# Four stage edits in a one-core decoder block: branch weights pair by pair, half of the merged columns kept on chip, partial sums added where they form, Strassen pairs moved

## The chip, the core and the metric

The kernel runs on one core of a Trainium2 chip. A core has a matrix engine (PE, TensorE), a vector engine (DVE), an activation engine (ACT), GpSimd (POOL), a queue engine (SP) that here only issues DMAs, an on-chip memory (SBUF) and the matmul's accumulators (PSUM). Each engine runs its own instruction stream in order; semaphores tie the streams together. The metric is the device time of one execution in microseconds; the median of several runs counts.

## The reference

One layer of a hybrid decoder, 256 tokens, width 2048, float32. What the change touches is the second half of it:

```python
gates = jax.nn.sigmoid(gz + b_gate[l]).reshape(B, S, N_BRANCH, D_MODEL)
mixed = gates[:, :, 0] * (branches[0] @ w_branch[l, 0])
for n in range(1, N_BRANCH):
    mixed = mixed + gates[:, :, n] * (branches[n] @ w_branch[l, n])
h = h + mixed @ w_out[l]
v = rms_norm(h, norm_ffn[l])
h = h + (jax.nn.silu(v @ w_ffn_gate[l]) * (v @ w_ffn_up[l])) @ w_ffn_down[l]
return rms_norm(h, norm_final)
```

Ahead of it the input is normed and projected (`w_in`), and four token mixers (two attentions, a linear recurrence, a windowed attention) give the four `branches`, each 256 x 512. `w_branch` is 4 x 512 x 2048, `w_out` 2048 x 2048, `w_ffn_gate` and `w_ffn_up` 2048 x 5632, `w_ffn_down` 5632 x 2048.

## The kernel before

**Numbers.** Each float32 operand is split into a high and a low part (`whi`, `wlo` for weights, `yh`, `yl` and the like for activations), and a product is three matmuls: high weight with high activation, low with high, high with low. A weight piece is 256 rows x 512 columns, loaded as `raw` by SP, its high part made by ACT (`whi<-raw`), its low part by DVE (`wlo<-raw,whi`). Four buffers each of `raw`, `whi` and `wlo` go round (`wpiece`, line 118).

**`pair`** (line 245) multiplies the 256 tokens (two row halves t) with two 512-column weight blocks (wl, wr) and walks the contraction in pairs kp of 128-row blocks. A normal kp is 8 products, 24 matmuls. A kp listed in `skps` is done as one Strassen step: 7 products, 21 matmuls, but `s_weights` (line 220) then forms sums of the weights first: four adds of 128x512 (`se`, `sx`), a high part (`sh`, `seh`, ACT) and a low part (`sl`, `sel`, DVE). Four of its products gather in their own banks p1, p5, p6, p7; at the last Strassen kp they are put together as the partial sum `u` (lines 284 to 291). The plain products gather in q0 and q1. With `split=n` the last n normal kps are held back and written product by product for the four outputs one after the other (lines 297 to 307), pinned in that order by `keep_in_program_order`. `small_banks` puts the four outputs in p1, p5, p7, p6 instead of q0 and q1.

**Stages.** From about 427 us on six times a gate block (`pair` on `w_in`, 8 kps) and a branch block (`pair` on `w_branch`, two kps, line 813) alternate; DVE multiplies gate and branch and adds to `mixed`. Then `w_out` in two column halves (line 864), 11 blocks of gate and up projection of the FFN (line 887, f = 0 to 10), the down projection `w_fd` in two halves cc (line 932, 22 kps each) and the final norm. Between stages, 128x128 transposes on PE turn a result round (`trans_bank`). The transposed `mixed` goes out to DRAM through `nat_out` (`mrg`, issued by POOL) and comes back in `m_split` (`mload`, issued by SP) as the activations `mth`, `mtl` of `w_out`. Such work is put in the list `later` and written out by `run_later`, at kp 1 of the next `pair` (line 272) or at its last Strassen kp.

**Order.** The code is written under a tile scheduler, which orders each engine's stream itself; only what is pinned keeps its place. So the order in the streams is not that of the code.

Of the kernel before, what the change touches and what calls it, by code (L numbers as in the profile page):

```python
# [10 lines left out]
AF = mybir.ActivationFunctionType  # L11
# [6 lines left out]
NKT = D // P  # L18
# [11 lines left out]
def hybrid_block_kernel(  # L30
# [213 lines left out]

    def pair(wl, wr, nkp, skps, a_of, upool=None, split=0, small_banks=False):

# [24 lines left out]
        for kp in range(nkp):  # L271
            if kp == 1 and (not skps or skps[0] > 1) and not small_banks:
                run_later()
            blk, sums = a_of(kp, kp in skps)
            if kp in skps:
# [525 lines left out]
    for n, cc in ((2, 0), (0, 0), (1, 1), (3, 1), (2, 1), (0, 1)):  # L801
# [5 lines left out]
        for t in range(2):  # L807
# [5 lines left out]
        pp, _ = pair(w_branch[n, :, col:col + 512], w_branch[n, :, col + 512:col + 1024], 2, (),  # L813
                     a_tiles(*ys[n]), split=2, small_banks=True)
        for i in range(2):
            if n == 1:
                mixed_of[2 * cc + i] = gp.tile([P, 2, 512], F32, tag="mixed", name="mixed")
        for t in range(2):
            for i in range(2):
                g, m = gate[:, 2 * t + i, :], mixed_of[2 * cc + i][:, t, :]  # L820
                tt(m if n == 1 else g, g, pp[t][i], ALU.mult)
                if n != 1:
                    tt(m, m, g, ALU.add)
        if n == 0:
            for i in range(2):
                later.append(lambda c=2 * cc + i: nat_out(mixed_of[c], merged, f"mrg{c}_"))
    s2.close()
# [17 lines left out]
    m_of = a_tiles(mth, mtl)  # L845

    def m_split(kp, s):
        if kp % 2 == 0:
            late["m"] = fp.tile([P, 2, 512], F32, tag="hd", name="mload")
        v = late["m"][:, kp % 2, :]  # L850
        nc.sync.dma_start(v, merged[kp])
        h, lo = (t[:, 2 * kp:2 * kp + 2, :].rearrange("p a b -> p (a b)") for t in (mth, mtl))
        act(h, v)
        tt(lo, v, rd(h), ALU.subtract)
        return m_of(kp, s)

# [28 lines left out]
    for f in range(DFF // 512):  # L885
        fs = slice(f * 512, (f + 1) * 512)
        q, u = pair(w_fg[:, fs], w_fu[:, fs], NKT // 2, (3, 5) if f == 0 else FS if f % 2 else (0, 3, 5), v_of, fp, split=1)
        hd = fp.tile([P, 2, 512], F32, tag="hd", name="hd")
        for t in range(2):
            o = u[:, 2 * t:2 * t + 2, :]  # L890
            tt(o, o, q[t], ALU.add)
            act(u[:, 2 * t, :], u[:, 2 * t, :], AF.Silu, scale=rstd2[:, t:t + 1])

        tt(hd, u[:, 0:4:2, :], u[:, 1:4:2, :], ALU.mult)
        later.append(lambda hd=hd, f=f: nat_out(hd, hid, f"hid{f}_"))
# [9 lines left out]
    ah = uv.tile([P, 4, 2, 2 * S], F32R, tag="tl", name="ah")  # L905
    DS = (3, 6, 9, 12, 15)

# [22 lines left out]
    for cc in range(2):  # L930
        cs = slice(cc * 1024, (cc + 1) * 1024)
        q, u = pair(w_fd[:, cc * 1024:cc * 1024 + 512], w_fd[:, cc * 1024 + 512:(cc + 1) * 1024], NFT // 2, DS,
                    lambda kp, ws: h_of(cc, kp, ws), fp, split=2 if cc else 1)
        for t in range(2):
            o = hn[:, t, cs].rearrange("p (a b) -> p a b", a=2)
            stt(o, u[:, 2 * t:2 * t + 2, :], rstd2[:, t:t + 1], o, ALU.mult, ALU.add)
        for t in range(2):
# [61 lines left out]
```

## Time and profile before

| | before |
|---|---|
| median of three runs | 1542.94 us (1542.46, 1542.94, 1548.3) |
| profiled execution, its own time | 1541.55 us |
| its span, first to last instruction | 1539.8 us |
| PE busy | 97% of the span |
| DVE, ACT, POOL busy | 77%, 53%, 5% |
| mean granted TensorE clock | 0.992 of full speed |

The rows are read with these names: `q<-whi,ah` is a matmul into bank q with weight piece `whi` and activation `ah`; `[1.41 <-DVE wlo L60]` behind a row says that the engine sat idle 1.41 us before it, and that the last thing it waited for was DVE's `wlo`. Line 216 is every matmul of `pair`, line 60 every two-operand DVE instruction, line 57 every ACT instruction, so rows are told apart by their tiles. A matmul of 512 columns lasts 0.39 us in the rows, but the next one starts before it ends: the pace is the distance of starts. Where PE is nearly always busy, time is found in the places where this distance is larger.

### The profile page before, as it was taken

How to read it: one execution, taken by the hardware profiler on the slowest of the kernel's cores; microseconds unless marked ns; L12 is line 12 of the kernel's file. 1: busy time of each engine (PE TensorE's matmuls, PEld its weight loads, DVE VectorE, ACT ScalarE, POOL GpSimd, SP SyncE). 2: the span in 40 equal slices, each digit the busy share in tenths (PEclk: the TensorE clock that was granted, in tenths of full speed). 3: DMA queues.
4: the chain of work that ended last, by engine and by line, in shares of the span. 5: the costliest groups of instructions: out<-in, count | busy, mean ns of one | idle time of the engine just before them, and what ended most of it. 6: DMA issues, size and time to landing. Idle time of an engine off the chain costs nothing.

```text
span 1539.8 us, 18550 instructions
## 1 busy us (share of the span) xinstructions
PE 1499.9 (97%) x6772; PEld 1231.3 (80%) x6772; DVE 1193.1 (77%) x1391; ACT 820.4 (53%) x947; POOL 76.7 (5%) x99
## 2 busy tenths in 40 slices
PE   8999999999999999998998999999999999999997
PEld 7878888887877877786887888888888888887885
DVE  5756645769679668765567989999999999898775
ACT  5555844545444444443465655564555556664643
POOL 4000300001000000000000000000000000001001
PEclk9999999999999999999999999999999999999999
DMA  7655555567566666666657567666766668876663
GB/s 237 214 150 158 154 172 159 171 176 255 167 196 208 222 201 196 191 184 219 225 177 246 177 195 256 199 215 193 234 200 220 201 221 269 280 263 216 212 209 110
DMA packets 159499, 313.64 MB, mean 204 GB/s; under 512 B 10736, under 2 KB 12848, under 8 KB 159280
## 3 DMA queue, kind: packets, MB, share of 16 engines
q1 hardware_dynamic: 155104, 298.92, 61.7%
q0 software_dynamic: 4272, 13.54, 2.5%
q8 instruction: 53, 0.87, 0.2%
q14 instruction: 38, 0.31, 0.1%
q10 hardware_dynamic: 32, 0.01, 0.0%
HBM read 302.46 MB, written 9.96 MB: 203 GB/s over the span
## 4 chain that ended last, share of the span: by engine, by line
PE 89%; DVE 3%; issue 3%; DMA 2%; ACT 1%; POOL 0%; SPq 0%; POOLq 0%; ACTq 0%; DVEq 0%
PE q L216 51%; PE acc L133 20%; PE p L216 14%; PE ps L165 2%; DMA sx<-in_w_in_dram 1%; DVE wlo L60 1%; DVE sl L60 1%; ACT sh L57 1%; DMA mload<-mrg 0%; DMA xq<-in_x_dram 0%; PE ps L533 0%; PE ps L729 0%; PE ps L552 0%; DMA fin<-hid 0%; PE ps L491 0%
## 5 line engine op out<-in xcount | busy, mean ns | idle before, releaser
L60 DVE TENSOR_TENSOR wlo<-raw,whi 128x1024 fp32r<-128x1024 f32 (+1 forms) x418 | 510.1, 1225 | 216.7 <-ACT whi L57 213.7
L57 ACT ACTIVATE whi<-raw 128x1024 fp32r<-128x1024 f32 (+1 forms) x418 | 438.2, 1050 | 438.1 <-PE q L216 252.8
L133 PE MATMUL acc<-wlo,uth 128*128 128x512 f32 (+1 forms) x448 | 173.4, 390 | 0.0
L133 PE MATMUL acc<-whi,utl 128*128 128x512 f32 (+1 forms) x448 | 173.4, 388 | 0.0
L133 PE MATMUL acc<-whi,uth 128*128 128x512 f32 (+1 forms) x448 | 168.0, 391 | 0.6 <-DVE nat L64 0.4
L216 PE MATMUL q<-whi,ah 128*128 128x512 f32 x512 | 161.1, 392 | 3.0 <-DVE hn L68 2.5
L216 PE MATMUL q<-whi,vth 128*128 128x512 f32 x408 | 159.6, 392 | 0.0
L216 PE MATMUL q<-wlo,vth 128*128 128x512 f32 x408 | 159.0, 390 | 0.0
L216 PE MATMUL q<-whi,vtl 128*128 128x512 f32 x408 | 158.7, 391 | 0.0
L57 ACT ACTIVATE sh<-sx 128x2048 fp32r<-128x2048 f32 x59 | 112.9, 1914 | 82.2 <-issue 34.6
L60 DVE TENSOR_TENSOR sl<-sx,sh 128x2048 fp32r<-128x2048 f32 x59 | 135.0, 2287 | 26.3 <-ACT sh L57 26.3
L216 PEld LDWEIGHTS q<-whi,ah 128*128 128x128 f32 x512 | 96.8, 189 | 24.1 <-DVE hn L68 3.0
L216 PE MATMUL q<-whi,uth 128*128 128x512 f32 x288 | 112.5, 394 | 2.4 <-DVE gate L60 2.4
L216 PE MATMUL q<-wlo,uth 128*128 128x512 f32 x288 | 113.2, 393 | 0.0
L216 PE MATMUL q<-whi,utl 128*128 128x512 f32 x288 | 112.7, 391 | 0.0
L60 DVE TENSOR_TENSOR sel<-se,seh 128x1536 fp32r<-128x1536 f32 x59 | 103.4, 1752 | 7.8 <-ACT seh L57 7.8
L57 ACT ACTIVATE seh<-se 128x1536 fp32r<-128x1536 f32 x59 | 87.3, 1480 | 36.4 <-DVE se L60 36.2
L216 PE MATMUL q<-wlo,ah 128*128 128x512 f32 x256 | 100.3, 392 | 0.0
L133 PEld LDWEIGHTS acc<-wlo,uth 128*128 128x128 f32 x448 | 84.6, 189 | 16.9 <-issue 1.0
L133 PEld LDWEIGHTS acc<-whi,utl 128*128 128x128 f32 x448 | 84.5, 189 | 16.4 <-issue 0.7
L133 PEld LDWEIGHTS acc<-whi,uth 128*128 128x128 f32 x448 | 82.1, 189 | 16.9 <-issue 0.7
L216 PEld LDWEIGHTS q<-whi,vtl 128*128 128x128 f32 x408 | 76.6, 188 | 15.9
(384 smaller groups left out, 2531.8 us busy)
## 6 DMA issues: line engine op xcount, KB each, us to landing
raw<-in_w_in_dram SPq DMA_DIRECT2D x168, 512.0 KB, 3.6
raw<-in_w_ffn_down_dram SPq DMA_DIRECT2D x68, 512.0 KB, 5.1
raw<-in_w_ffn_gate_dram SPq DMA_DIRECT2D x51, 512.0 KB, 3.8
raw<-in_w_ffn_up_dram SPq DMA_DIRECT2D x51, 512.0 KB, 4.6
sx<-in_w_ffn_up_dram SPq DMA_DIRECT2D x37, 512.0 KB, 3.9
sx<-in_w_ffn_gate_dram SPq DMA_DIRECT2D x37, 512.0 KB, 4.8
raw<-in_w_branch_dram SPq DMA_DIRECT2D x32, 512.0 KB, 4.3
raw<-in_w_out_dram SPq DMA_DIRECT2D x32, 512.0 KB, 4.7
```

Of the source, the lines that this page charges most:

```text
L57: return nc.scalar.activation(o, i, f, **kw)
L60: return (eng or nc.vector).tensor_tensor(out=o, in0=a, in1=b, op=op)
L133: m = nc.tensor.matmul(acc, x_, w_, start=st, stop=sp_)
L165: nc.tensor.transpose(pt[:, i * S + t * P:i * S + (t + 1) * P], nat[:, t, (c0 + i) * P:(c0 + i + 1) * P], ident)
L216: m = nc.tensor.matmul(acc, x_, w_, start=st, stop=sp_)
```

## The change

It has five parts.

1. The branch block drops `split=2`: its two kps are written kp by kp, and nothing there is pinned any more.
2. Merged columns 2 and 3 (`mixed_of[2]`, `mixed_of[3]`, ready last) no longer go through DRAM: `to_T` transposes them and writes `mth` and `mtl` straight from PSUM (`mth<-ps`, `mtl<-ps`), and `m_split` returns them for kp 4 to 7. From `w_out` on, `run_later` comes at kp 2 instead of kp 1.
3. The first FFN block, f = 0, has no Strassen kp any more (before: kp 3 and 5). Its result then is only in q: ACT applies Silu from PSUM and DVE multiplies with the other half.
4. The two `pair`s on `w_fd` get a sixth Strassen kp, 18.
5. `hn` gets the partial sum `u` where `u` is formed (`at_mid`) instead of behind the `pair`.

```diff
-    late = {"psum": None, "turn": 0}
+    late = {"psum": None, "turn": 0, "at": 1}
...
-            if kp == 1 and (not skps or skps[0] > 1) and not small_banks:
+            if kp == late["at"] and (not skps or skps[0] > kp) and not small_banks:
                 run_later()
...
                     tt(u[:, 1:4:2, :], p[5].unsqueeze(1).to_broadcast([P, 2, 512]), u[:, 1:3, :], ALU.subtract)
+                    if at_mid is not None:
+                        at_mid(u)
                     run_later()
...
         pp, _ = pair(w_branch[n, :, col:col + 512], w_branch[n, :, col + 512:col + 1024], 2, (),
-                     a_tiles(*ys[n]), split=2, small_banks=True)
+                     a_tiles(*ys[n]), small_banks=True)
...
-        if n == 0:
-            for i in range(2):
-                later.append(lambda c=2 * cc + i: nat_out(mixed_of[c], merged, f"mrg{c}_"))
+        if n == 0 and cc == 0:
+            for c in range(2):
+                later.append(lambda c=c: nat_out(mixed_of[c], merged, f"mrg{c}_"))
...
+    for c in (2, 3):
+        later.append(lambda c=c: to_T(mixed_of[c], mth, mtl, 4 * c))
+
     def m_split(kp, s):
+        if kp > 3:
+            return m_of(kp, s)
...
+    late["at"] = 2
...
-        q, u = pair(w_fg[:, fs], w_fu[:, fs], NKT // 2, (3, 5) if f == 0 else FS if f % 2 else (0, 3, 5), v_of, fp, split=1)
+        q, u = pair(w_fg[:, fs], w_fu[:, fs], NKT // 2, () if f == 0 else FS if f % 2 else (0, 3, 5), v_of, fp, split=1)
...
+        if u is None:
+            for t in range(2):
+                act(hd[:, t, :], q[t][:, 0, :], AF.Silu, scale=rstd2[:, t:t + 1])
+                tt(hd[:, t, :], hd[:, t, :], q[t][:, 1, :], ALU.mult)
...
-    DS = (3, 6, 9, 12, 15)
+    DS = (3, 6, 9, 12, 15, 18)
...
+        def at_mid(u):
+            for t in range(2):
+                o = hn[:, t, cs].rearrange("p (a b) -> p a b", a=2)
+                stt(o, u[:, 2 * t:2 * t + 2, :], rstd2[:, t:t + 1], o, ALU.mult, ALU.add)
+
...
-                    lambda kp, ws: h_of(cc, kp, ws), fp, split=2 if cc else 1)
-        for t in range(2):
-            o = hn[:, t, cs].rearrange("p (a b) -> p a b", a=2)
-            stt(o, u[:, 2 * t:2 * t + 2, :], rstd2[:, t:t + 1], o, ALU.mult, ALU.add)
+                    lambda kp, ws: h_of(cc, kp, ws), fp, split=2 if cc else 1, at_mid=at_mid)
```

Up to the first branch block the streams of all engines are the same. PE has as many instructions as before (6688): six matmuls more in f = 0, three fewer in each `w_fd` pair. Four DMAs less are issued by POOL (`mrg`) and four less by SP (`mload`).

**PE, first branch block, before.** p1, p5, p7, p6 are the four outputs; pieces 4070 and 4076 are the left and right block of kp 0, 4082 and 4088 those of kp 1. The block's 4th to 9th matmul:

```order
L216 MATMUL p1_4064<-whi_4070,yh_2536 128x512
L216 MATMUL p1_4064<-wlo_4071,yh_2536 128x512
L216 MATMUL p1_4064<-whi_4070,yl_2537 128x512
L216 MATMUL p1_4064<-whi_4082,yh_2536 128x512
L216 MATMUL p1_4064<-wlo_4083,yh_2536 128x512
L216 MATMUL p1_4064<-whi_4082,yl_2537 128x512
```

The first matmul on a kp 1 piece is the 7th of the block, the first on its low part the 8th.

**PE, first branch block, after** (4070 and 4076 as before, 4106 and 4112 are the pieces of kp 1), the block's 22nd to 30th matmul:

```order
L216 MATMUL p6_4067<-whi_4076,yh_2536 128x512
L216 MATMUL p6_4067<-wlo_4077,yh_2536 128x512
L216 MATMUL p6_4067<-whi_4076,yl_2537 128x512
L216 MATMUL p1_4064<-whi_4106,yh_2536 128x512
L216 MATMUL p5_4065<-whi_4112,yh_2536 128x512
L216 MATMUL p7_4066<-whi_4106,yh_2536 128x512
L216 MATMUL p6_4067<-whi_4112,yh_2536 128x512
L216 MATMUL p1_4064<-wlo_4107,yh_2536 128x512
L216 MATMUL p1_4064<-whi_4106,yl_2537 128x512
```

A kp 1 piece is now first read by the 25th matmul, its low part by the 29th. DVE's stream around it is the same as before up to the low parts of kp 1.

**DVE, start of `w_out`, before.** `mixed_4566` is merged column 3, `mload_5773` and `mload_5884` the reloaded halves for kp 0 and 1, and for kp 2 and 3; `wlo_5891` and `wlo_5897` are the low parts of kp 2's weights, `wlo_5857` of kp 1's:

```order
L60 TENSOR_TENSOR wlo_5857<-raw_5854,whi_5856 128x1024
L60 TENSOR_TENSOR mixed_4566<-mixed_4566,u_5583 128x512
L60 TENSOR_TENSOR mtl_5766<-mload_5773,mth_5765 128x512 x2
L60 TENSOR_TENSOR wlo_5891<-raw_5888,whi_5890 128x1024
L60 TENSOR_TENSOR wlo_5897<-raw_5894,whi_5896 128x1024
L60 TENSOR_TENSOR mtl_5766<-mload_5884,mth_5765 128x512
```

**The same place after** (`wlo_5825` belongs to kp 1, `wlo_5887` and `wlo_5893` to kp 2, `mload_5880` to kp 2 and 3):

```order
L60 TENSOR_TENSOR wlo_5825<-raw_5822,whi_5824 128x1024
L60 TENSOR_TENSOR mixed_4566<-mixed_4566,u_5583 128x512
L60 TENSOR_TENSOR mtl_5766<-ps_5852,mth_5765 128x512
L60 TENSOR_TENSOR mtl_5766<-ps_5859,mth_5765 128x512
L60 TENSOR_TENSOR mtl_5766<-mload_5773,mth_5765 128x512
L60 TENSOR_TENSOR mtl_5766<-ps_5866,mth_5765 128x512
L60 TENSOR_TENSOR mtl_5766<-mload_5773,mth_5765 128x512
L60 TENSOR_TENSOR mtl_5766<-ps_5873,mth_5765 128x512
L60 TENSOR_TENSOR mtl_5766<-mload_5880,mth_5765 128x512
L60 TENSOR_TENSOR wlo_5887<-raw_5884,whi_5886 128x1024
L60 TENSOR_TENSOR mtl_5766<-mload_5880,mth_5765 128x512
L60 TENSOR_TENSOR wlo_5893<-raw_5890,whi_5892 128x1024
```

The low part of kp 2's activations, and with it the wait for the second reload, has moved ahead of kp 2's weights; ACT's stream is changed in the same way. On PE all 16 transposes stand ahead of the first `w_out` matmul in both kernels.

**DVE, change from the first to the second half of `w_fd`, before.** `hn<-q0` and `hn<-q1` empty the two accumulators of half 0; `wlo_10993` and `wlo_10999` are the pieces of its last kp 21, `wlo_11044` to `wlo_11083` pieces of half 1; `fin` and `ah` are the loaded hidden activations, their sums and low parts:

```order
L60 TENSOR_TENSOR wlo_10993<-raw_10990,whi_10992 128x1024
L60 TENSOR_TENSOR wlo_10999<-raw_10996,whi_10998 128x1024
L60 TENSOR_TENSOR wlo_11044<-raw_11041,whi_11043 128x1024
L60 TENSOR_TENSOR ah_10109<-fin_10106,ah_10109 128x512
L60 TENSOR_TENSOR wlo_11050<-raw_11047,whi_11049 128x1024
L68 SCALAR_TENSOR_TENSOR hn_5756<-q0_10110,rstd2_6489,hn_5756 128x1024
L60 TENSOR_TENSOR fin_10106<-fin_10106 128x128 x2
L60 TENSOR_TENSOR ah_10109<-fin_10106,ah_10109 128x512
L60 TENSOR_TENSOR fin_10106<-fin_10106 128x128
L60 TENSOR_TENSOR wlo_11083<-raw_11080,whi_11082 128x1024
L60 TENSOR_TENSOR fin_10106<-fin_10106 128x128
L68 SCALAR_TENSOR_TENSOR hn_5756<-q1_10111,rstd2_6489,hn_5756 128x1024
```

**The same place after** (`sel_11276` belongs to half 1's second Strassen kp, `wlo_10972` and `wlo_10978` to kp 21, `wlo_11021` to `wlo_11060` to half 1):

```order
L60 TENSOR_TENSOR sel_11276<-se_11272,seh_11275 128x1536
L60 TENSOR_TENSOR wlo_10972<-raw_10969,whi_10971 128x1024
L60 TENSOR_TENSOR wlo_10978<-raw_10975,whi_10977 128x1024
L60 TENSOR_TENSOR se_11396<-sx_11393 128x512
L60 TENSOR_TENSOR wlo_11021<-raw_11018,whi_11020 128x1024
L60 TENSOR_TENSOR ah_10079<-fin_10076,ah_10079 128x512
L60 TENSOR_TENSOR sx_11393<-sx_11393 128x512
L60 TENSOR_TENSOR wlo_11027<-raw_11024,whi_11026 128x1024
L68 SCALAR_TENSOR_TENSOR hn_5756<-q0_10080,rstd2_6471,hn_5756 128x1024
L60 TENSOR_TENSOR se_11396<-sx_11393 128x512
L60 TENSOR_TENSOR wlo_11060<-raw_11057,whi_11059 128x1024
L68 SCALAR_TENSOR_TENSOR hn_5756<-q1_10081,rstd2_6471,hn_5756 128x1024
```

The sums of half 1's `fin`, which need a loaded tile, have moved from ahead of `hn<-q1` to behind it; kp 21's pieces stand directly behind the Strassen work for half 1.

## Rows read from the trace of the kernel before

**Rows 1.** The page: the span, and busy time by engine.

```profile
span 1539.8 us, 18550 instructions
...
PE 1499.9 (97%) x6772; PEld 1231.3 (80%) x6772; DVE 1193.1 (77%) x1391; ACT 820.4 (53%) x947; POOL 76.7 (5%) x99
```

**Rows 2.** Timeline of PE, first and sixth branch block: start, length, instruction, wait.

```profile
427.29 0.39 PE L216 MATMUL p<-whi,yh 128*128 128x512 f32 x1
...
428.65 0.39 PE L216 MATMUL p<-whi,yh 128*128 128x512 f32 x1
430.44 0.50 PE L216 MATMUL p<-wlo,yh 128*128 128x512 f32 x1 [1.41 <-DVE wlo L60]
...
440.04 0.40 PE L216 MATMUL p<-sh,uth 128*128 128x512 f32 x1
...
705.08 0.39 PE L216 MATMUL p<-whi,yh 128*128 128x512 f32 x1
...
715.96 0.49 PE L165 MATMUL ps<-ident,mixed 128*128 128x128 f32 x3
```

**Rows 3.** Timeline of DVE, first branch block: first low part of its second pair.

```profile
429.17 1.22 DVE L60 TENSOR_TENSOR wlo<-raw,whi 128x1024 fp32r<-128x1024 f32 x1
```

**Rows 4.** Timeline at the start of `w_out`: SP and PE.

```profile
716.57 0.93 SPq L851 DMA_DIRECT2D mload<-mrg  x2
...
724.24 0.80 PE L216 MATMUL q<-whi,mth 128*128 128x512 f32 x1 [3.06 <-ACT mth L57]
```

**Rows 5.** Timeline of PE, FFN block f = 0, around its first Strassen pair.

```profile
835.66 0.39 PE L216 MATMUL q<-whi,vtl 128*128 128x512 f32 x1
839.74 0.47 PE L216 MATMUL p<-sh,vth 128*128 128x512 f32 x1 [3.69 <-issue]
...
841.74 1.22 PE L216 MATMUL p<-seh,vsh 128*128 128x512 f32 x2 [1.06 <-ACT seh L57]
...
845.08 0.39 PE L216 MATMUL q<-sh,vtl 128*128 128x512 f32 x1
```

**Rows 6.** Timeline of PE, first matmul of `w_fd`.

```profile
1290.28 0.47 PE L216 MATMUL q<-whi,vsh 128*128 128x512 f32 x1 [0.75 <-DVE u L60]
```

**Rows 7.** Timeline of all engines, change between the halves of `w_fd`.

```profile
1410.78 0.39 PE L216 MATMUL p<-sh,ah 128*128 128x512 f32 x1
...
1411.15 2.35 POOL L60 TENSOR_TENSOR hn<-hn,fin 128x1024 f32<-128x1024 f32 x1 [104.60 <-ACT junk L57]
1411.21 2.45 DVE L60 TENSOR_TENSOR fin<-fin 128x128 f32<-128x128 f32 x1
...
1414.91 0.79 PE L216 MATMUL q<-whi,ah 128*128 128x512 f32 x1 [2.53 <-DVE hn L68]
...
1418.37 0.62 PE L216 MATMUL q<-whi,ah 128*128 128x512 f32 x2
```

**Rows 8.** DVE's groups by form, 1306 to 1386 us: count, busy, mean ns.

```profile
L60 DVE TENSOR_TENSOR wlo<-raw,whi 128x1024 fp32r<-128x1024 f32 x20 | 24.4, 1219 | 3.6 <-ACT whi L57 3.6
L60 DVE TENSOR_TENSOR sl<-sx,sh 128x2048 fp32r<-128x2048 f32 x5 | 11.4, 2284 | 0.0
L60 DVE TENSOR_TENSOR sel<-se,seh 128x1536 fp32r<-128x1536 f32 x6 | 10.5, 1751 | 0.0
L60 DVE TENSOR_TENSOR ah<-fin,ah 128x512 fp32r<-128x512 f32 x15 | 10.3, 685 | 0.3 <-ACT ah L57 0.3
...
L60 DVE TENSOR_TENSOR fin<-fin 128x128 f32<-128x128 f32 x16 | 4.2, 285 | 0.8 <-DMA fin<-hid 0.8
```

**Rows 9.** One window of 16 us in half 0 of `w_fd`: length, PE, PEld, DVE, ACT, POOL busy, clock.

```profile
1370.00:1386.00 16.00, 16.00 (x72) 13.27 (x71) 15.90 (x17) 9.93 (x12) 0.00 (x0) 1.00 0.76 254
```

**Rows 10.** Timelines of DVE and PE where pair 16 of half 0 begins.

```profile
1367.08 1.22 DVE L60 TENSOR_TENSOR wlo<-raw,whi 128x1024 fp32r<-128x1024 f32 x1
1368.21 0.68 DVE L60 TENSOR_TENSOR ah<-fin,ah 128x512 fp32r<-128x512 f32 x1
...
1374.93 0.39 PE L216 MATMUL q<-whi,ah 128*128 128x512 f32 x1
```

More of the change, by code (lines that the diff above doesn't have):

```diff
@@ L243, in run_later, with pair @@
             later.pop(0)()
-    def pair(wl, wr, nkp, skps, a_of, upool=None, split=0, small_banks=False):
+    def pair(wl, wr, nkp, skps, a_of, upool=None, split=0, small_banks=False, at_mid=None):
         pq = late["psum"]
@@ L886, in hybrid_block_kernel @@
         fs = slice(f * 512, (f + 1) * 512)
-        q, u = pair(w_fg[:, fs], w_fu[:, fs], NKT // 2, (3, 5) if f == 0 else FS if f % 2 else (0, 3, 5), v_of, fp, split=1)
+        q, u = pair(w_fg[:, fs], w_fu[:, fs], NKT // 2, () if f == 0 else FS if f % 2 else (0, 3, 5), v_of, fp, split=1)
         hd = fp.tile([P, 2, 512], F32, tag="hd", name="hd")
-        for t in range(2):
[L890 to L894, printed above, removed]
+        if u is None:
+            for t in range(2):
+                act(hd[:, t, :], q[t][:, 0, :], AF.Silu, scale=rstd2[:, t:t + 1])
+                tt(hd[:, t, :], hd[:, t, :], q[t][:, 1, :], ALU.mult)
+        else:
+            for t in range(2):
+                o = u[:, 2 * t:2 * t + 2, :]
+                tt(o, o, q[t], ALU.add)
+                act(u[:, 2 * t, :], u[:, 2 * t, :], AF.Silu, scale=rstd2[:, t:t + 1])
+            tt(hd, u[:, 0:4:2, :], u[:, 1:4:2, :], ALU.mult)
         later.append(lambda hd=hd, f=f: nat_out(hd, hid, f"hid{f}_"))
@@ L931, in hybrid_block_kernel @@
         cs = slice(cc * 1024, (cc + 1) * 1024)
+        def at_mid(u):
+            for t in range(2):
+                o = hn[:, t, cs].rearrange("p (a b) -> p a b", a=2)
+                stt(o, u[:, 2 * t:2 * t + 2, :], rstd2[:, t:t + 1], o, ALU.mult, ALU.add)
         q, u = pair(w_fd[:, cc * 1024:cc * 1024 + 512], w_fd[:, cc * 1024 + 512:(cc + 1) * 1024], NFT // 2, DS,
-                    lambda kp, ws: h_of(cc, kp, ws), fp, split=2 if cc else 1)
-        for t in range(2):
-            o = hn[:, t, cs].rearrange("p (a b) -> p a b", a=2)
-            stt(o, u[:, 2 * t:2 * t + 2, :], rstd2[:, t:t + 1], o, ALU.mult, ALU.add)
+                    lambda kp, ws: h_of(cc, kp, ws), fp, split=2 if cc else 1, at_mid=at_mid)
         for t in range(2):
```

## The prediction

> **What bounds the kernel now.** First the page: PE is busy 97% of 1539.8 us and no other engine over 77% [rows 1]. So time is won in two ways only: fewer matmuls, or closing a place where PE stands. For the second I looked along PE's timeline for starts further apart than the usual pace, and at each such place for what ended last. The usual pace comes from the sixth branch block, which has no stall: 48 matmuls from 705.08 to 715.96 are 10.88 us, 0.2267 us each [rows 2]. Places that the change touches: the first five branch blocks (DVE's low part is late), the start of `w_out` (a reload from DRAM), the first Strassen pair of FFN block 0, the first matmul of `w_fd`, and the change between its halves [rows 2, 4 to 7]. I call a pair of 256 contraction rows kp, as the code does.
>
> The sum below is made against the profiled execution, 1541.55 us. The median of the three runs lies 1.4 above it, and I add that at the end.
>
> **Branch blocks, −9.2.** In block 1 PE waits 1.41 us for the low part of kp 1's left piece: it is DVE's instruction from 429.17 to 430.39, and PE asks for it at the 8th matmul [rows 2, 3]. The whole block lasts from 427.29 to 440.04, 12.75 us, where 48 matmuls need 10.88: 1.87 lost. The other stalled blocks lose 1.84, 1.87, 1.79 and 1.80 read in the same way; together 9.2. After the change DVE's stream up to that instruction is the same, but PE asks for it at the 29th matmul only, 427.29 + 28 x 0.2267 = 433.64, so 3.2 us after it is there. The right piece's low part stands two instructions of about 1.2 us later and is asked for still later. Nothing new comes in front: the next gate block's pieces reuse the buffers of kp 0, which are now let go earlier. The output products finish closer together at the block's end, and DVE must multiply the four of them then (8 instructions of about 0.69, the size of `ah` [rows 8]); the next block needs those banks only at its kp 2, some 48 matmuls on, 10.9 us. Bounds: −7.0 (only the 1.41 waits go, five times) and −9.2. I take −9.2, because block 6, with the low parts early, runs at 10.88 with no loss at all.
>
> **Start of `w_out`, 0.** PE's first matmul waits 3.06 us for `mth`, which waits for the reload that SP issued at 716.57 [rows 4]. The change removes the DRAM trip of columns 2 and 3, but kp 0 needs column 0, and this is still reloaded, still issued behind the load of x, which waits for the last branch matmul. The 16 transposes stand in front of `w_out` as before and need the last `mixed`, for which DVE has the same work. So the wait stays. Better by up to 3.06 if four stores and later reloads less on the queues let the tile land sooner; worse if the extra weight load that SP now issues ahead of it is still under way, by its transfer time, about 1.5. Zero lies between, and the order of the two loads that decide is unchanged.
>
> **FFN block 0, −6.7 + 1.4 = −5.3.** At its first Strassen kp PE goes from 835.66 to 845.08 with 12 starts between, 9.42 us where 12 x 0.2267 = 2.72 are needed [rows 5]: the waits of 3.69 and 1.06 and a wider spacing behind them. 6.7 us are lost, because the sums of the first Strassen weights of the stage can begin late only. Without Strassen kps this goes; two kps with 24 instead of 21 matmuls cost 6 x 0.2267 = 1.36. Does it come back one block later? In the new order the sums for block 1's first Strassen kp stand in block 0, and the first matmul on them is the 139th of the stage, not the 89th as before: 11 us more time for a chain of four adds, `sh` and `sl`, that comes late by 3.69 now. I take no loss; the bound is the same stall again, +6.7. The new evacuation is two ACT and two DVE instructions per block and lies under kp 0 and 1 of block 1, which begins on the other accumulator's banks as soon as half is done.
>
> **First matmul of `w_fd`, −0.8.** The wait of 0.75 for `u` [rows 6] goes, since in the new order DVE does this step ahead of the weights in its place; the margin is 0.2 us, so bounds 0 and −0.8.
>
> **Sixth Strassen pair, −1.4 on PE.** Twice 3 matmuls, 6 x 0.2267 = 1.36. Its price is on DVE: four adds at 0.685, `sl` 2.28, `sel` 1.75, four small sums at 0.285 and a low part at 0.685 come in, two `wlo` at 1.22 go out [rows 8]: 2.74 + 2.28 + 1.75 + 1.14 + 0.69 − 2.44 = 6.2 us more per half. In half 1 the tail leaves room. In half 0 DVE is busy 15.90 of 16 us already [rows 9], so there I followed it from 1367.08, where it makes kp 16's first low part, to kp 21's second, in the new order. That is ten `wlo`, six `ah`, eight adds, two `sl`, two `sel`, four small sums, one `vsl`, and the steps for `u` and `hn` (two of 0.685, three of `wlo`'s size): 12.2 + 4.1 + 5.5 + 4.6 + 3.5 + 1.1 + 0.7 + 1.4 + 3.7 = 36.8 us. An instruction starts some 0.08 before the one ahead of it ends (1367.08 + 1.22 against 1368.21 [rows 10]); over 38 instructions that takes off 3.0, so 33.8. PE begins kp 16 at 1374.93 [rows 10] and asks for that piece 124 matmuls later, at 1403.0: 35.9 us. So the piece is there between 2.1 us early and 0.9 late.
>
> **Change between the halves, −4.0.** From 1410.78 to 1418.37 PE does 11 starts in 7.59 us where 2.49 would do: 5.1 lost. The longest wait, 2.53, is for DVE's `hn<-q1` [rows 7], which stood behind a 0.285 us sum of `fin` that took 2.45 [rows 7, 8]. After the change the sums of `fin` stand behind `hn<-q1`. `hn<-q1` then ends, by the same walk, about 0.5 us ahead of q1's first matmul. So the whole 5.1 can go, but margins are under 2 us on either side; I take back 1.1, near the late end of the walk. Bounds 0 and −5.1.
>
> The 2.45 us sum ran while POOL multiplied `hn` for 2.35, from 1411.15 [rows 7]. The Trainium skill (SBUF — State Buffer, "SBUF: two separate sides") says that a vector instruction with two SBUF inputs and a GpSimd instruction that reads SBUF exclude each other for the whole instruction. The trace agrees: 2.45 instead of 0.285. By that rule a `wlo` behind a starting POOL multiply would be held as long as the sum was, while `hn<-q1`, with one input in PSUM, would not; if the first multiply fell ahead of `wlo_11060` the sum of this part would be −4.0 + 2.4, which is within rival 1.
>
> Of its own, the earlier addition of `u` moves nothing: the streams before already have those two instructions right behind `u`. The final norm is untouched.
>
> **Sum.** −9.2 + 0 − 5.3 − 0.8 − 1.4 − 4.0 = −20.7; 1541.55 − 20.7 = 1520.9; plus 1.4 for the median: 1522.3.
>
> **Rivals.** 1: *DVE becomes the bound at the end of half 0.* For it: 15.90 of 16 busy [rows 9], 6.2 us more work, a walk with margins of 1 us, two POOL multiplies of 2.35 and more [rows 7]. Against it: 6.2 is met by the lead of a whole Strassen kp. Then the 5.1 stay and up to the 2.4 of one POOL hold is added: 1522.3 + 4.0 to 1522.3 + 6.4, 1526 to 1529. Chance 0.15.
>
> 2: *The reload of kp 2 takes the place of that of kp 0 at `w_out`.* kp 2's weights now stand behind the second reload on ACT and DVE. For it: the new order. Against it: four stores less ahead of it on the queues. It decides if that tile lands over 1 us later than before; the price is at most a second wait like 3.06 and the two splits that follow it, one `whi` and one `wlo`, 2.3: up to 5.4, so 1524 to 1528. Chance 0.10.
>
> 3: *The branch change moves the wait instead of removing it*, to the next gate block, whose weights compete with the four multiplications. Half of 9.2 comes back: 1527. Against it: the margin of 3.2 us. Chance 0.08.
>
> 4, the other side: *the odd FFN blocks stall.* With the Strassen kps of block 0 gone, the order of the blocks behind it is another: in blocks 1, 3, 5, 7, 9 the matmuls between the last use of a `sel` buffer and the first use of its next content fall from 48 or more to 37, 8.4 us. `sl` 2.28, `sel` 1.75 and two `wlo`, 2.4 [rows 8] queue in that time on DVE, 6.5. If two more of `wlo`'s size get ahead, 8.9, each of the five blocks waits; at a cost as at 835.66, 6.7 each [rows 5], this is +33.5 and 1556. Against it: the whole of blocks 1 to 10 has no wait of note in the trace now. Chance 0.04.
>
> That the change doesn't do what it says is true of its last part (above) and costs nothing.
>
> **How the numbers follow.** The forecast (all terms near what I took) has 0.57, the rivals 0.15, 0.10, 0.08 and 0.04, and 0.06 is for two of the first three together or a stall that I haven't seen, 1530 to 1545. A measurement of this kernel tells about 0.5% from no change, 7.7 us: faster means under 1535.2. Forecast and rivals 1 to 3 are faster, 0.90, less 0.03 for larger prices than mine: 0.87; same 0.09, slower 0.04. Range: down to 1515 (`w_out`'s 3.1, the 1.1 taken back and some 3 us by which runs of one kernel differ), up to 1532, which is rival 1 at its full price with a second wait of 3.1 at `w_out`, 1522.3 + 6.4 + 3.1; rival 4 and most of the unseen are left out.
>
> **What would show it.** Right: five branch blocks of 10.9 us without a wait for `wlo`; no wait at FFN block 0's kps; less than 1.5 us lost between 1390 and 1400 at the change of halves; the 3 us wait at `w_out` still there. Wrong: a PE wait for `wlo` or `hn` near the end of half 0 (rival 1), one for `whi` or `mth` some 48 matmuls into `w_out` (rival 2), waits for `sel` or `seh` in blocks 1, 3, 5 (rival 4).

## The result and the profile after

The changed kernel takes 1531.08 us (median of four runs, 1530.25 to 1531.35) against 1545.26 of the kernel before in the same runs; the ratio is 0.9897, with an interval of 0.9879 to 0.9916. That is 14.2 us between the medians (15.9 by the ratio), where 20.6 were forecast; the measured 1531.1 lies inside the stated range, 1515 to 1532, by 0.9 us. From profile to profile the change is 10.6 us (1541.55 to 1530.98), since the profiled execution of before was one of its shorter ones.

Page of the changed kernel, span and busy time by engine; PE stands at 98% [before: rows 1]:

```profile
span 1529.3 us, 18519 instructions
...
PE 1497.3 (98%) x6772; PEld 1230.8 (80%) x6772; DVE 1191.7 (78%) x1397; ACT 817.0 (53%) x944; POOL 74.4 (5%) x95
```

Where the time went is read from the starts of named matmuls in both traces, stage by stage:

| stretch on PE | before | after | change | predicted |
|---|---|---|---|---|
| start to first branch matmul | 427.29 | 427.44 | +0.2 | 0 |
| first to last branch matmul | 288.44 | 279.18 | −9.3 | −9.2 |
| last branch matmul to first `w_out` matmul | 8.51 | 9.51 | +1.0 | 0 |
| `w_out`, to the first FFN matmul | 93.48 | 93.81 | +0.3 | 0 |
| FFN, to the first `w_fd` matmul | 472.56 | 466.34 | −6.2 | −6.1 |
| `w_fd`, first to last matmul | 238.50 | 241.56 | +3.1 | −5.4 |
| behind the last matmul | 11.1 | 11.4 | +0.4 | 0 |

So two large terms came out as forecast, and one, `w_fd`, missed by 8.5 us. PE's waits in the changed kernel from 380 to 620 us answer rows 2 and 3 (columns: who waits for whom, us in total, times, longest). The four waits for `wlo` of the branch blocks in this stretch are gone, and behind it, to 716 us, there is none either; the one wait that is left stands ahead of the stage, as it did before:

```profile
PE q L216 <- DVE gate L60: 2.4, 1, 2.4
```

The same view from 830 to 1290 us, where rows 5 and 6 stood, has no line. At the start of `w_out` the wait of rows 4 is still there, a little longer (timeline of PE; start, length, instruction, wait):

```profile
716.13 0.79 PE L216 MATMUL q<-whi,mth 128*128 128x512 f32 x1 [3.27 <-ACT mth L57]
716.72 0.63 PE L216 MATMUL q<-wlo,mth 128*128 128x512 f32 x1
717.15 0.63 PE L216 MATMUL q<-whi,mth 128*128 128x512 f32 x1
```

Behind the wait the matmuls start 0.43 us apart instead of 0.227. The granted clock is 1.00 from 700 to 711 us, where the branch matmuls end and PE waits between transposes, and 0.50 from 712 to 721 us, which is the lower of its two levels, 1.2 GHz; from 722 us on it is 1.00 again.

In `w_fd` PE now stands for low parts of weights before the end of half 0, and at the change of halves (rows 7) one wait of 0.81 us is left. Timeline of PE:

```profile
1361.04 0.39 PE L216 MATMUL q<-whi,ah 128*128 128x512 f32 x1
1362.27 0.50 PE L216 MATMUL q<-wlo,ah 128*128 128x512 f32 x1 [0.84 <-DVE wlo L60]
...
1364.61 0.50 PE L216 MATMUL q<-wlo,ah 128*128 128x512 f32 x1 [0.69 <-DVE wlo L60]
...
1392.62 0.50 PE L216 MATMUL q<-wlo,ah 128*128 128x512 f32 x1 [2.54 <-DVE wlo L60]
...
1403.55 0.50 PE L216 MATMUL p<-sh,ah 128*128 128x512 f32 x1 [0.81 <-ACT ah L57]
```

This looks like rival 1, DVE as the bound at the end of half 0. But DVE's own waits in half 0 say that it had stood idle before. In the changed kernel (1276 to 1400 us):

```profile
DVE fin L60 <- DMA fin<-hid: 10.5, 3, 3.7
DVE wlo L60 <- ACT whi L57: 4.2, 2, 4.0
```

and in the kernel before (1290 to 1412 us):

```profile
DVE wlo L60 <- ACT whi L57: 6.3, 5, 3.6
DVE fin L60 <- DMA fin<-hid: 2.9, 2, 2.1
DVE ah L60 <- ACT ah L57: 1.0, 3, 0.5
```

DVE stood three times, 3.2 to 3.7 us each, for a hidden tile that SP loads. The third of these in the changed kernel, DVE and SP:

```profile
1349.06 0.68 DVE L60 TENSOR_TENSOR ah<-fin,ah 128x512 fp32r<-128x512 f32 x1
1349.66 1.22 DVE L60 TENSOR_TENSOR wlo<-raw,whi 128x1024 fp32r<-128x1024 f32 x1
1350.79 0.68 DVE L60 TENSOR_TENSOR se<-se,sx 128x512 f32<-128x512 f32 x1
1354.99 1.02 DVE L60 TENSOR_TENSOR fin<-fin 128x128 f32<-128x128 f32 x4 [3.51 <-DMA fin<-hid]
1355.93 2.28 DVE L60 TENSOR_TENSOR sl<-sx,sh 128x2048 fp32r<-128x2048 f32 x1
...
1361.00 1.22 DVE L60 TENSOR_TENSOR wlo<-raw,whi 128x1024 fp32r<-128x1024 f32 x1
```

```profile
1349.77 0.34 SPq L927 DMA_DIRECT2D fin<-hid  x1
```

The low part `ah` at 1349.06 is the last reader of one of three buffers for hidden tiles. It ends at 1349.74, SP issues the next load at 1349.77, and DVE goes on with the tile at 1354.99, 5.2 us after the issue. DVE's stream has only two instructions between the release and the four sums that need the tile, and behind the sums stand `sl`, `sel` and the `wlo` at 1361.00 that PE is late for. In the kernel before the four sums stand apart, between `sl`, `sel` and low parts. DVE before:

```profile
1346.94 2.28 DVE L60 TENSOR_TENSOR sl<-sx,sh 128x2048 fp32r<-128x2048 f32 x1
1350.04 0.49 DVE L60 TENSOR_TENSOR fin<-fin 128x128 f32<-128x128 f32 x2 [0.82 <-DMA fin<-hid]
...
1351.65 0.28 DVE L60 TENSOR_TENSOR fin<-fin 128x128 f32<-128x128 f32 x1
...
1352.99 0.28 DVE L60 TENSOR_TENSOR fin<-fin 128x128 f32<-128x128 f32 x1
1353.19 1.75 DVE L60 TENSOR_TENSOR sel<-se,seh 128x1536 fp32r<-128x1536 f32 x1
```

The `wlo` at 1361.00 is the first low part of kp 16, and the matmul at 1361.04 is the first of kp 16. So DVE's lead over PE at this place, the start of the one to the start of the other, is 0.04 us; in the kernel before it was 7.85 (1367.08 and 1374.93 [rows 10]). From 1354.99 to 1402.5 us DVE then has no idle time, and PE waits for it.

### The profile page after: what moved, and what is told of

The parts are those of the page before. It is cut to its first block, busy times and chain, and to the rows that moved or that the text cites. A ratio compares the mean times of both kernels' runs of the same rounds, so it can differ in the third digit from the quotient of the medians.

```text
span 1529.3 us, 18519 instructions
## 1 busy us (share of the span) xinstructions
PE 1497.3 (98%) x6772; PEld 1230.8 (80%) x6772; DVE 1191.7 (78%) x1397; ACT 817.0 (53%) x944; POOL 74.4 (5%) x95
## 4 chain that ended last, share of the span: by engine, by line
PE 90%; DVE 4%; DMA 3%; issue 2%; ACT 0%; POOL 0%; SPq 0%; POOLq 0%; ACTq 0%; DVEq 0%
PE q L216 52%; PE acc L133 20%; PE p L216 14%; PE ps L165 2%; DMA fin<-hid 1%; DVE wlo L60 1%; DMA mload<-mrg 1%; DMA xq<-in_x_dram 1%; DVE sel L60 1%; DVE ah L60 0%; DVE se L60 0%; DMA raw<-in_w_in_dram 0%; PE ps L535 0%; PE ps L731 0%; PE ps L554 0%
## 5 line engine op out<-in xcount | busy, mean ns | idle before, releaser
L216 PE MATMUL q<-wlo,vth 128*128 128x512 f32 x424 | 165.8, 391 | 0.0
L216 PE MATMUL q<-whi,vtl 128*128 128x512 f32 x424 | 165.6, 391 | 0.0
L216 PE MATMUL q<-whi,vth 128*128 128x512 f32 x424 | 164.5, 391 | 0.0
L216 PE MATMUL q<-whi,ah 128*128 128x512 f32 x480 | 151.4, 392 | 0.0
L216 PEld LDWEIGHTS q<-whi,ah 128*128 128x128 f32 x480 | 90.8, 189 | 18.9
L216 PE MATMUL q<-wlo,ah 128*128 128x512 f32 x240 | 94.9, 395 | 4.9 <-DVE wlo L60 4.8
L216 PEld LDWEIGHTS q<-whi,vth 128*128 128x128 f32 x424 | 79.6, 188 | 16.3
```

The costliest lines, as they stand in the source:

```text
L216: m = nc.tensor.matmul(acc, x_, w_, start=st, stop=sp_)
```

## The experiments

The runs are compared by what `w_fd` loses in each. A loss is the sum of the distances between matmul starts in a stretch, less 0.2267 us for each (the dense pace of rows 2). The stretches are counted from the first `w_fd` matmul: the start is 0 to 20 us, half 0 is 20 to 117, the change of halves 117 to 135, half 1 from 135 on. The first column is DVE's lead at kp 16, taken as above.

| kernel | lead at kp 16 | start | half 0 | change | half 1 | `w_fd`, first to last matmul |
|---|---|---|---|---|---|---|
| before | 7.9 | 1.0 | 0.0 | 5.1 | 0.0 | 238.50 |
| branch blocks alone | 7.6 | 1.0 | 0.2 | 5.7 | 0.0 | 239.24 |
| merged columns alone | 7.7 | 2.3 | 0.1 | 6.2 | 0.0 | 240.97 |
| f = 0 edit alone | 5.2 | 1.0 | 5.1 | 4.9 | 0.0 | 243.41 |
| sixth pair alone | 5.2 | 2.0 | 0.4 | 1.6 | 2.5 | 237.47 |
| changed kernel | 0.0 | 1.0 | 5.1 | 2.8 | 1.7 | 241.56 |
| changed, reload first | 1.5 | 1.0 | 3.5 | 2.5 | 3.5 | 241.55 |
| changed, five pairs | 6.0 | 1.2 | 1.8 | 4.7 | 0.0 | 239.95 |
| changed, fourth buffer | 8.5 | 1.2 | 0.0 | 2.3 | 0.0 | 234.41 |
| changed, both | 8.5 | 1.0 | 0.0 | 2.3 | 0.0 | 234.23 |
| both, five pairs | 8.9 | 1.0 | 0.2 | 0.0 | 0.0 | 233.52 |
| f = 0 edit, fourth buffer | 8.9 | 1.0 | 0.2 | 0.0 | 0.0 | 233.54 |
| before, fourth buffer | 8.8 | 1.0 | 3.0 | 0.0 | 0.0 | 236.39 |
| before, no GpSimd multiply | 7.6 | 2.0 | 0.2 | 4.0 | 0.0 | 238.61 |

The losses of the changed kernel sum to 10.6 against 6.1; with 1.4 us of matmuls less that is the 3 us by which its `w_fd` is longer.

Some of these kernels have the same order of DVE's instructions in `w_fd`, and so show how far two executions of one order lie apart: the first three rows (238.50 to 240.97 us), the changed kernel with and without the reload first (241.56, 241.55), and the f = 0 edit alone and the changed kernel with five pairs (243.41, 239.95). So a single length of `w_fd` is good to some 3 us only. Where the loss lies repeats: in half 0 it is 0.2 or less with the order of before, 1.8 and 5.1 with that of the f = 0 edit, 3.5 and 5.1 with that of the changed kernel.

Two theories of the miss in `w_fd`. **Theory 1, the tile wait:** the edit of FFN block 0 lets the scheduler put the four sums together and right behind the release of their buffer, so DVE loses its lead to a load. **Theory 2, the work:** the sixth Strassen pair's 6.2 us of DVE work per half overrun it (rival 1 as it was meant). Four runs do one part of the change alone, on the kernel before. The kernel before ran beside them at 1545.8 us (23 runs).

**Branch blocks alone.**

```diff
-                     a_tiles(*ys[n]), split=2, small_banks=True)
+                     a_tiles(*ys[n]), small_banks=True)
```

> The kernel before with one edit: the branch blocks written kp by kp. If the prediction's step holds, the five stalled blocks of 12.7 us become 10.9 us, PE's waits for wlo there go, and the whole is 9.2 us shorter, with nothing else changed. Rival (the wait moves to the next gate block): half of it, 4 to 5 us, comes back as PE waits between 440 and 720 us.

1536.84 us, ratio 0.9939 (0.9918 to 0.9960), which of 1545.8 is 9.4 us less. From the first to the last branch matmul it is 279.17 us, against 288.44 before. The step holds in mechanism and size, and nothing comes back in the gate blocks. Rival 3 is out.

**Merged columns alone.**

```diff
-        if n == 0:
+        if n == 0 and cc == 0:
...
+    for c in (2, 3):
+        later.append(lambda c=c: to_T(mixed_of[c], mth, mtl, 4 * c))
...
+        if kp > 3:
+            return m_of(kp, s)
...
+    late["at"] = 2
```

> The kernel before with one edit: merged columns 2 and 3 kept on chip (and the deferred work at kp 2 from w_out on). If the start of w_out is set by the reload of column 0 alone, PE's wait of 3.06 us before the first w_out matmul stays within 0.5 us and the total is the same within 2 us. Rival: four stores and four reloads less on the queues let the tile land earlier, 2 to 3 us gained there. Other rival: kp 2's weights behind the second reload cost a new wait of 1 us or more some 48 matmuls into w_out.

1547.42 us, ratio 1.0008 (0.9993 to 1.0022): no change. From the last branch matmul to the first of `w_out` it is 8.57 us, against 8.51 before, and no wait follows in `w_out`, so kp 2's weights behind the second reload are in time: rival 2 is out. The other rival, 2 to 3 us gained by an earlier reload, isn't seen in the time. The traces don't exclude a smaller gain: in five other kernels with before's order at that place the way took 9.7 to 10.5 us.

There is one cost that the prediction didn't have. In FFN block 0, where rows 5 stood, PE's waits of 3.69 and 1.06 are one of 6.4 us here, and the FFN takes 474.96 us instead of 472.56. The edit also moves the deferred work to kp 2 there; that this is the reason was not tried. In the changed kernel block 0 has no Strassen kp, and this cost isn't in it.

**FFN block 0 without Strassen alone.**

```diff
-... (3, 5) if f == 0 else FS if f % 2 else (0, 3, 5), v_of, fp, split=1)
+... () if f == 0 else FS if f % 2 else (0, 3, 5), v_of, fp, split=1)
```

> The kernel before with one edit: no Strassen pair in FFN block 0. FFN block 0 to first w_fd matmul: 6 us shorter by the prediction. For w_fd there are two theories of why the changed kernel loses 3 us there instead of gaining 5. Theory 1 (tile wait): this edit alone makes the scheduler put the four sums of the loaded hidden tile right behind the release of its buffer, so DVE waits over 3 us each for the load twice in half 0, as in the changed kernel; but with five Strassen pairs only, there is room behind them, so w_fd is within 2 us of before. Theory 2 (work): DVE's waits for the tile are a side matter; w_fd is as before within 1 us and so is its loss of 5.1 us at the change of halves.

1540.88 us, ratio 0.9966 (0.9950 to 0.9981), 5.3 us less by the ratio. The FFN is 6.2 us shorter, 466.35. But `w_fd`, in which no line was touched, is 243.41 us, 4.9 longer than before, and DVE again waits for hidden tiles (1287 to 1410 us):

```profile
DVE fin L60 <- DMA fin<-hid: 9.2, 3, 4.2
DVE wlo L60 <- ACT whi L57: 9.0, 7, 4.3
```

The order is theory 1's, with two waits over 3 us in half 0, 3.25 and 4.18; the third of this view, 1.79, lies at the change of halves. The changed kernel has the same two, and as a third the one shown above, which stands at the four sums of the sixth pair. That there would be room behind two waits with five pairs was wrong: half 0 loses as much as in the changed kernel, PE waiting 0.6 and 2.3 us for `wlo`, and the loss at the change of halves is still there.

The time says less than this profile. The edit gains 5.3 us by the ratio (some 2.4 either way), and the FFN alone explains 6.2, so about 1 us is left for `w_fd`, and not 4.9; the profiled execution, 1542.90 us, is one of the longer of eight (1537.76 to 1544.88).

**The sixth Strassen pair alone.**

```diff
-    DS = (3, 6, 9, 12, 15)
+    DS = (3, 6, 9, 12, 15, 18)
```

> The kernel before with one edit: the sixth Strassen pair, 18, in w_fd. Theory 1 (tile wait): DVE's order here interleaves the sums with other work, so DVE waits under 3 us for hidden tiles in half 0, keeps its lead, and w_fd is 1 to 6 us shorter than before. Theory 2 (work): the 6.2 us more DVE work alone overrun half 0; PE waits for wlo near its end as in the changed kernel, and w_fd is 2 to 4 us longer than before.

1546.24 us, ratio 1.0000 (0.9985 to 1.0015). `w_fd` is 237.47 us, 1.0 less than before, the least that theory 1 expected, and in time nothing is gained. DVE waits 2.4 us for hidden tiles in half 0 (1294 to 1412 us):

```profile
DVE wlo L60 <- ACT whi L57: 3.5, 1, 3.5
DVE fin L60 <- DMA fin<-hid: 2.4, 2, 2.1
DVE sl L60 <- ACT sh L57: 1.1, 1, 1.1
```

So the sixth pair alone does not overrun half 0, as theory 2 had it: half 0 loses 0.4 there, where the changed kernel loses 5.1. But the pair isn't free. It takes as much of the lead at kp 16 as the f = 0 edit does, to 5.2 us from 7.9; neither edit alone brings it to 0.0. The loss at the change of halves is 1.6 instead of 5.1, and half 1 loses 2.5 that it didn't lose. There DVE waits for hidden tiles longer than before (14.7 us in four waits against 10.0 in three). With a fourth buffer for these tiles half 1 loses nothing, though the sixth pair's work is still there.

By their ratios the parts are −9.4, +1.2, −5.3 and 0.0 us, together −13.5; the whole change is −15.9 by its ratio, with an interval of some 3 us either way. In time nothing but the sum of the parts is seen. In the traces two parts do meet: the 2.4 us that the merged columns cost in FFN block 0 fall away with the f = 0 edit, and the sixth pair meets the f = 0 edit in half 0.

Four more runs start from the changed kernel (1531.08); the kernel before ran beside them at 1545.39. The changed kernel itself did not, so differences to it are between medians, with the difference by the ratios to the kernel before in brackets; the latter have 4 to 5 us either way.

**A fourth buffer for hidden tiles.**

```diff
-            v = fin[:, D + kp % 3 * 512:D + (kp % 3 + 1) * 512]
+            v = fin[:, D + kp % 4 * 512:D + (kp % 4 + 1) * 512]
...
-                   fin[:, D + 1536:].rearrange("p (a b) -> p a b", a=4))
+                   wsum[:, 0, :].rearrange("p (a b) -> p a b", a=4))
```

with `wsum` in the buffer of `hd`, which is free by then.

> The changed kernel with four instead of three buffers for the loaded hidden tiles of w_fd (the scratch of the sums moves to a free tile). Theory 1 (tile wait): the loads start one pair earlier, DVE's waits for hidden tiles in half 0 fall from 10.5 us to under 3, PE's waits for wlo there go, and w_fd (241.6 us from its first to its last matmul) becomes 234 to 238; the total is 4 to 8 us below the changed kernel. Theory 2 (work of the sixth Strassen pair): DVE is still too late near the end of half 0, w_fd stays at 240 or above.

1522.97 us (1521.79 to 1523.71), ratio 0.9855 (0.9831 to 0.9878), 8.1 below the changed kernel (6.5). `w_fd` is 234.41 us. DVE's waits for the loaded tile in half 0 (1275 to 1400 us; the sums now read as `wsum`):

```profile
DVE wlo L60 <- ACT whi L57: 2.9, 2, 2.0
DVE vsl L60 <- ACT vsh L57: 2.1, 3, 0.7
DVE wsum L60 <- DMA fin<-hid: 1.1, 2, 0.9
```

The waits and `w_fd` are what theory 1 expected, and the total is at the edge of it (4 to 8). The sixth pair's work is still in it, and DVE's lead at kp 16 is 8.5 us. One reservation: the edit also changes DVE's order, and the four sums stand apart again, in twos and ones. So the runs with the fourth buffer show what `w_fd` costs without the tile waits; they do not separate the buffer from the order.

**The changed kernel with five Strassen pairs.**

```diff
-    DS = (3, 6, 9, 12, 15, 18)
+    DS = (3, 6, 9, 12, 15)
```

> The changed kernel without the sixth Strassen pair (five, as before). Theory 1: the order behind the f = 0 edit stays, DVE still waits over 3 us twice for hidden tiles, w_fd is 242 to 244 us, 0 to 2 us longer than in the changed kernel. Theory 2: with 6.2 us less DVE work in half 0 the loss there goes and w_fd is under 239.5 us.

1530.25 us (1528.3 to 1532.62), ratio 0.9903 (0.9877 to 0.9930): the same as the changed kernel within the intervals. `w_fd` is 239.95 us, between the two theories' numbers; DVE's waits for hidden tiles are 7.0 us in 3 waits from 1260 to 1410 us, the longest 3.0, so both are less than theory 1 expected. The loss of 4.7 at the change of halves is back, as in every kernel here with five pairs and three buffers: the sixth pair is what moved it, not the earlier addition of `u`. Half 0 loses 1.8 where the f = 0 edit alone, with the same order on DVE, lost 5.1, so this run does not settle between the two theories' numbers. Leaving the sixth pair out costs the changed kernel no time that these runs show, where 1.4 us and more were forecast for it.

**The reload ahead of the load of x.**

```diff
-        nc.sync.dma_start(hn[:, :, cs], x[:, cs].rearrange("(t p) n -> p t n", p=P))
         q, _ = pair(w_out[...
                     m_of if cc else m_split, split=1)
+        nc.sync.dma_start(hn[:, :, cs], x[:, cs].rearrange("(t p) n -> p t n", p=P))
```

> The changed kernel with the load of x for w_out issued behind the first reload of merged columns instead of ahead of it. If the reload lands late because a load of 1 MB stands ahead of it on the queues, PE's wait of 3.3 us before the first w_out matmul falls under 1 us, its slow-clock stretch gets shorter, and the total is 2 to 5 us lower. Rival: the reload takes its time whatever stands ahead of it, and the wait stays within 0.7 us.

1526.50 us (1525.9 to 1527.32), ratio 0.9879 (0.9855 to 0.9902), 4.6 below the changed kernel (2.8). SP's issues in the changed kernel, and then in this one, with PE's first matmul:

```profile
707.04 0.37 SPq L872 DMA_DIRECT2D hn<-in_x_dram  x1
707.46 0.94 SPq L859 DMA_DIRECT2D mload<-mrg  x2
```

```profile
707.40 0.82 SPq L859 DMA_DIRECT2D mload<-mrg  x2
708.27 0.94 SPq L874 DMA_DIRECT2D hn<-in_x_dram  x2
```

```profile
712.42 0.74 PE L216 MATMUL q<-whi,mth 128*128 128x512 f32 x1
```

The reload is issued hardly earlier, 0.43 us behind the last branch matmul instead of 0.84, but ahead of the 1 MB load. ACT begins to split the reloaded tile 4.72 us behind that matmul instead of 8.83. The first `w_out` matmul follows the last branch matmul by 5.45 us instead of 9.51 and has no wait any more; what is left are the transposes and their waits for `mixed`. The granted clock of 712 to 721 us is 0.81 instead of 0.50. The load of x ahead of the reload was the cause, in the trace by 4.1 us; in time the ratios' intervals overlap.

**Both.**

> Both edits, the fourth buffer and the reload first. If the two losses are separate, their gains add: 6 to 13 us below the changed kernel. If one hides the other, it is within 1.5 us of the better of the two.

The edits are those of the two runs above. 1519.55 us (1518.77 to 1520.31), ratio 0.9832 (0.9804 to 0.9860): 11.5 below the changed kernel (10.0), where 8.1 + 4.6 = 12.7 would be the sum. `w_fd` is 234.23 us, the way to `w_out` 5.45, as in the two runs of one edit: the two losses are separate.

The last four ran with the kernel before at 1545.2 beside them.

**GpSimd's hold at the change of halves,** on the kernel before:

```diff
                 sumsq(ss3[:, t, 0:1], o, 1024)
-                tt(o, o, gfin[:, cs], ALU.mult, nc.gpsimd)
                 continue
```

> The kernel before without GpSimd's two multiplications of half 0 of hn by the final norm's weights (left out of the computation). All other instructions keep their order. If the 2.45 us sum at the change of halves was held by GpSimd, it now takes 0.3 us, DVE's hn<-q1 ends about 2 us earlier and PE's wait for it falls from 2.5 us to under 1; the loss of 5.1 us at the change becomes 1.5 to 3.5. Rival: DVE is late there for its own work, the sum stays above 1 us or the wait stays at 2 us or more.

1541.77 us, ratio 0.9971 (0.9958 to 0.9983), 3.4 less between the medians. The same sum that took 2.45 us [rows 7], and the `hn<-q1` behind it, in timeline of DVE:

```profile
1414.88 0.29 DVE L60 TENSOR_TENSOR fin<-fin 128x128 f32<-128x128 f32 x1
1415.08 1.28 DVE L68 SCALAR_TENSOR_TENSOR hn<-q,rstd,hn 128x1024 f32<-128x1024 f32 x1
```

PE's wait for `hn` is 0.4 us, not 2.5. With GpSimd's instruction gone the sum takes 0.29. So the hold that the prediction read from rows 7, and for which it cited the Trainium skill (SBUF — State Buffer, "SBUF: two separate sides"), is shown by this run. But the loss at the change falls only to 4.0, from 5.1 to 6.2 in the three kernels with before's order, less than expected: PE's wait for `ah`, that is for a hidden tile, grew from 0.48 to 1.28 us, and a stretch with the granted clock at 0.50 still follows the waits. The hold was one of several things that were late at the same place. Where the rest of the 3.4 us lies was not found; the profiled execution of before is a short one.

**The f = 0 edit with the fourth buffer,** on the kernel before, the edits as above.

> The kernel before with no Strassen pair in FFN block 0 and with four buffers for the hidden tiles. Theory 1 (tile wait): w_fd, 243.4 us with that edit alone, falls to 239 or less, and the total is 8 to 13 us below the kernel before. Rival: the f = 0 edit costs w_fd its 4.9 us by other work moved into it, and w_fd stays above 241.

1533.87 us, ratio 0.9919 (0.9904 to 0.9934), 11.3 less than before. `w_fd` is 233.54 us where the f = 0 edit alone gave 243.41, and DVE has no wait over 0.9 us for a tile in half 0; from 20 us on `w_fd` loses 0.2 us. This is theory 1 without the sixth pair, with the same reservation on the order.

**The best version with five pairs.**

> The fourth buffer and the reload first, with five Strassen pairs instead of six. With DVE's tile waits gone, the sixth pair should be worth its 1.4 us of matmuls or a little more: w_fd 235 to 237.5 us here against 234.2 with six. If the sixth pair's 6.2 us of DVE work still cost PE anything, this kernel is the faster by 1 us or more.

1518.15 us (1516.85 to 1519.03), ratio 0.9817 (0.9802 to 0.9831). `w_fd` is 233.52 us against 234.23 with six. The expectation, 235 to 237.5, was wrong: with no tile waits left in the way the sixth pair saves nothing. In time the two can't be told apart (1518.15 and 1519.55, intervals overlap). With six pairs and the fourth buffer both traces have one PE wait in `w_fd`, at the change of halves, which those with the f = 0 edit and five pairs don't have (PE's waits in the run with both edits, 1260 to 1540 us):

```profile
PE p L216 <- ACT vsh L57: 2.0, 1, 2.0
```

It is more than the 1.4 us of matmuls that the pair saves. What makes ACT late there was not tried.

**The fourth buffer on the kernel before.**

> The kernel before with four buffers for the hidden tiles. DVE waits for them only 2.9 us in half 0 there, with no PE wait behind it. If the fourth buffer mends what the f = 0 edit spoiled and nothing else, the total is the same within 2 us and w_fd within 2 us of 238.5; if it helps by itself (by another order at the change of halves), w_fd is 233 to 236.

1543.54 us, ratio 0.9988 (0.9977 to 0.9998), 1.7 less between the medians; `w_fd` is 236.39 us, 2.1 less, at the edge of what was expected. The loss of 5.1 at the change of halves is gone in its trace, and 3.0 us are lost early in half 0. So the fourth buffer brings 1.7 us to the kernel before, 7.0 between medians to the one with the f = 0 edit alone and 8.1 to the changed kernel: most of it is the mending of what the f = 0 edit did.

## Why the prediction was right or wrong, step by step

- *Branch blocks, −9.2:* right, −9.3 in the traces and −9.4 by the ratio when timed alone. The order gave the mechanism (8th against 29th matmul), the block without a stall gave the size.
- *Start of `w_out`, 0:* right as a term (+1.0 between the two profiles, 1.2 longer in time when run alone, with an interval from 1.1 shorter to 3.4 longer), and for the stated reason, that the reload of column 0 stays. But I had left the cause of the wait at "still issued behind the load of x" without pricing it: in the trace it was worth 4.1 us to whoever swaps the two. The 8.51 us from the last branch to the first `w_out` matmul was also on the short side, against 9.7 to 10.5 in five other kernels with before's order. This is part of why the timed gain, 14.2, is larger than that between the profiles, 10.6.
- *FFN block 0, −5.3, and the first `w_fd` matmul, −0.8:* right, −6.2 together. The stall did not come back in block 1, and the odd blocks did not stall; PE has no wait from 830 to 1290 us, so rival 4 is out.
- *Change between the halves, −4.0:* the step held in part: the loss fell from 5.1 to 2.8 us, and PE's wait for `hn<-q1` is gone, by way of the sixth pair (with five it is 4.7). Of the 2.8 us, 1.0 is a wait of its own, for ACT's `ah` (1402.34 to 1403.55 instead of 0.23 for the next start); the rest lies behind the wait of 2.54 at the end of half 0, where the granted clock is 0.50 from 1394 to 1397 us.
- *Sixth pair, −1.4:* here the prediction failed, in two sentences. The first is that kp 21's second piece "is there between 2.1 us early and 0.9 late"; for its first piece PE waited 2.54 us already. The sum of the durations was not the error: from 1361.00 to the end of kp 21's second low part, 1393.70, DVE took 32.7 us, where 33.8 were forecast. The error is the start. The walk began at 1367.08, a row of the kernel before, and took DVE's lead of that row, 7.85 us, for the changed kernel, where it is 0.04. DVE had lost it in three waits of 3.2 to 3.7 us for a loaded tile. Two of them are there with the f = 0 edit alone, some 450 us upstream in the program, and the third is at the sixth pair's own sums; either edit alone leaves 5.2 us of the lead, both together 0.04 (1.53 in the run with the reload first, whose order on DVE is the same). The second is that "in half 1 the tail leaves room": half 1 loses 1.7 us in the changed kernel, 2.5 with the sixth pair alone. Against the forecast of −5.4 for `w_fd`, 5.1 of the missing 8.5 us lie in half 0, and 1.7 each in half 1 and, against the 1.1 taken back there, at the change.
- *Rival 1* had the likeliest chance of the others, 0.15, and its time, 1526 to 1529, is nearest to the result. Its sign came, a PE wait for `wlo` near the end of half 0 with DVE busy without a pause. Its reasons did not: half 0 holds the sixth pair's work without a loss where the tile waits are gone (0.0 with the fourth buffer) and loses 0.4 with the pair alone, and the 5.1 us at the change did not stay.
- *The range:* that 1531.1 lies inside it is luck as far as `w_fd` goes. Its upper end was rival 1 at its full price and a second wait at `w_out`, and neither was what cost the time. Of the signs of being right, "less than 1.5 us lost between 1390 and 1400" failed; the other three came.
- *What stays open:* why the scheduler groups the four sums when block 0 of the FFN is changed was not tried, nor was the fourth buffer with the sums left grouped. How much of the f = 0 edit's gain `w_fd` takes back is between 1 us (timed) and 4.9 (one profile). The earlier addition of `u` was not run alone; the streams of before have it in place already.

## What to carry to other kernels

Where a scheduler orders the streams, compare the order of every stage with the trace, not only of those that the edit names: look for a load's reader that has moved close behind the release of the load's buffer. A lead taken from a row of the old trace is only valid if the stream ahead of that row is the same. And before a stage's first load, ask which larger load stands ahead of it on the same queue and whether it is needed as early.

## What the runs showed of the hardware

A 256 KB load was issued 0.4 us earlier, counted from the last branch matmul, and ahead of a 1 MB load instead of behind it; ACT began to split it 4.1 us earlier, and PE's wait of 3.3 us for it went away altogether. A VectorE sum of 128x128 with two SBUF inputs took 2.45 us beside a GpSimd multiply and 0.29 us without it. Of the 5.1 us at the change of halves in the kernel before, 3.0 are waits; much of the rest are the matmuls behind them, 0.43 us apart instead of 0.227, where the granted clock is 0.50 (1415 to 1418 us). And not every idle engine is idle for want of work: in the same 80 us of `w_fd`, counted from its first matmul, DVE was busy 75.2 us before (1300 to 1380 us) and 65.1 in the changed kernel (1286 to 1366 us), where its three waits for a tile lie.
